# Strassen blocks of a down projection: one ring of five buffers, and the residual added in a later segment

## The chip, the cores and the metric

The kernel runs on one core of one Trainium2 chip. A core has five engines that work side by side and wait for each other through semaphores: TensorE (PE, matrix multiplies, results in PSUM), VectorE (DVE), ScalarE (ACT), GpSimd (POOL) and SyncE (SP). Here SP and POOL mostly start transfers (DMA). The metric is the device time of one execution in microseconds (us); lower is better.

## The reference

One layer of an encoder for two groups of 256 tokens (512 tokens together), model width 2048, in float32:

```python
h = h + mixed                                   # attention and delta-rule heads, projected by w_out
hn = rmsnorm(h, norm_ffn_w)
h = h + (jax.nn.silu(hn @ w_gate) * (hn @ w_up)) @ w_down      # D_FF = 5632
y = rmsnorm(h, final_norm_w)
```

Only the end matters here: the product with `w_down` (5632 x 2048), the residual `h` that is added to it, and the final norm.

## The kernel before

**Layout.** Everything is kept transposed: 128 rows of features on the partitions, the 512 tokens along the free dimension. `hT0` and `hT1` together hold the 16 row tiles of the result of the down projection; `hcol(j)` is a pair of them (128 x 1024), `hrow(i)` a single one. The 5632 rows of the hidden layer are 44 tiles, or 22 pairs, or 11 segments of four tiles. Before the down projection they lie in DRAM as 22 pairs (`s_act`), except segment 9, which stays in SBUF (`sA`); the residual lies there as `s_h2`.

**Precision.** A float32 weight tile is split into two parts that TensorE takes at full rate: ACT writes the rounded part `w_hi` (L134), DVE the rest `w_lo` (L135). Activations are split in the same way. All matmuls stand in a helper, so their line is always L82.

**Plain segments.** `down(s, a)` multiplies a segment: for each of eight columns j it loads a weight tile `w_raw` (L142, SP), splits it, runs 24 matmuls into two PSUM banks, and adds these to `hcol(j)` (L1140). The first segment copies instead (L1138), and after each column adds the residual by a transfer of POOL that accumulates into `hcol(j)` (`plus`, L967).

**Strassen groups.** 14 of the 22 pairs are multiplied in two groups of seven pairs (1792 rows). A group is eight blocks, and each block (`block`, also used by gate and up) makes one `hcol(j)` out of a 2 x 2 split of the weights (W11, W21, W12, W22, each 128 x 896 here) with seven products of 14 matmuls each, instead of eight. The sums of activations that the products need (`xd`) are made once for a group by `combine`: it loads a pair as `raw_a` (L1107, POOL), forms four differences and sums in `cmd` (L1108 to L1110, DVE), and splits both into `xd`. The seven combines run beside the first seven columns of the plain segment that comes before the group (`beside`).

The sums of weights are made in two buffers. SP loads W12 into `w_second` (L977) and W11 into `w_first` (L978); POOL adds W22 and W12 to them by accumulating transfers (L967). W11, W21 and W22 are also loaded as such (`b11`, `b21`, `b22`, L983 to L985, on the page all `b`). The seven products come in this order: b11 (PSUM bank ps_a), second (ps_c), first (ps_d), b21 (ps_a), first + b22 (ps_b; the sum is made in place by DVE, L1016), b22 (ps_d), first + b21 (ps_c; L1028). So `w_second` is last read by the second product's split, `w_first` by the last one's. The results go through `p1`, `p7` and `u2` into the block's output `out` (128 x 1024, L949 to L953, L1021, L1022), which DVE then adds to `hcol(j)` (L1149).

**Buffers.** In the pool `fq` of the down projection, `w_first` and `w_second` have a buffer each. A ring of three buffers of 4 KB a partition (`ring`) serves `raw_a`, `cmd`, `out` and, at the end, a part of the result. Gate and up alternate between two pools, each with its own `w_first` and `w_second`. The b tiles and `w_raw` share a ring of three; `w_hi` and `w_lo` have three each.

**Order of work.** The order of the matmuls is written out. All else is ordered by a planner before the kernel runs: each engine and each queue gets a fixed order, ranked by place in the program. `high_priority` moves instructions ahead in this ranking: by 120 instructions (`AHEAD`) for the splits of weights, by 360 for the loads and additions of `w_first`, `w_second` and the b tiles. A load whose buffer isn't free waits at the head of its queue, and what stands behind it on that queue waits too.

**The course of the down projection:** the plain segment 9 (with the combines of group 0 beside it and the residual added); `load_act` of segment 7, which loads two `raw_a` tiles (L1119, POOL) and splits them into the single buffer `sA`; group 0; the plain segment 7 (combines of group 1); `load_act` of segment 8; group 1; `load_act` of segment 10 into a buffer of its own; the plain segment 8; then segment 10 in two halves of tokens (`finish`), with the final norm.

Of the kernel before, what the change touches and what calls it, by code (L numbers as in the profile page):

```python
# [8 lines left out]
F32 = mybir.dt.float32  # L9
# [9 lines left out]
P = 128  # L19
# [14 lines left out]
GROUP = 7  # L34
NGROUP = 2
SEG0 = NGROUP * GROUP // 2
FIRST_SEG, MID_SEG, LAST_SEGS = 9, 7, (8, 10)
# [32 lines left out]
def hybrid_encoder(ctx: ExitStack, tc: tile.TileContext, xT, w_in, w_ba, w_out, w_gate,  # L70
# [153 lines left out]
    def sm_tile():  # L224
        return psm.tile([P, T], F32, tag="s", name="ps_s")
# [429 lines left out]
    state = {}  # L655
# [199 lines left out]
    pairs = [i for j in range(8) for i in (j, j + 8)]  # L855
# [37 lines left out]
    XC = [hp.tile([P, 7, 2, L], F32R, tag=f"xc{k}", name="xc") for k in range(8)]  # L893
    ga_cm = tc.tile_pool(name="gA", bufs=1, side="left", reuse_waits="tile")
    gA = ga_cm.__enter__()
    acc = gA.tile([P, T], F32, tag="acc", name="ssq_acc2")
    A11, S3, S1, A12, S2, S4, A22 = range(7)
    for n, i in enumerate(pairs):
        j = i % 8
# [62 lines left out]
    def ahead():  # L962
        return tc.high_priority(offset=AHEAD)

    def plus(dst, src):

        nc.gpsimd.dma_start(dst, src, accum_op=ALU.add)  # L967

    def block(w4, pool, xc, ix, p1_pool, new_out, opened=None):


        n = len(xc)
        w11, w21, w12, w22 = w4
        with tc.high_priority(offset=3 * AHEAD):
            first = pool.tile([P, n, P], F32, tag="first", name="w_first")
            second = pool.tile([P, n, P], F32, tag="second", name="w_second")
            nc.sync.dma_start(second, w12)  # L977
            nc.sync.dma_start(first, w11)  # L978
            plus(second, w22)
            plus(first, w12)  # L980
            b11, b21, b22 = [wp.tile([P, 8, P], F32, tag="raw", bufs=3, name=nm)[:, :n]
                             for nm in ("b11", "b21", "b22")]
            nc.sync.dma_start(b11, w11)  # L983
            nc.sync.dma_start(b21, w21)
            nc.sync.dma_start(b22, w22)  # L985

        def bank(pool_, tag, nm):
            return pool_.tile([P, T], F32, tag=tag, name=nm).rearrange("p (a t) -> p a t", a=2)

        pa, pb = bank(pg, "g", "ps_a"), bank(pso, "o0", "ps_b")  # L990
        pc, pd = bank(psm, "s", "ps_c"), bank(pso, "o1", "ps_d")
        with ahead():
            w = w_split(b11)
        product(pa, w, xc, ix[A11], True)
        if opened:
            opened()
        fp, out = state["fp"], new_out()
        p1 = p1_pool.tile([P, L], F32, tag="p1", name="p1")
        plus_both(p1, None, pa)
        with ahead():  # L1000
            w = w_split(second)
        product(pc, w, xc, ix[S3], True)
        p7 = fp.tile([P, 2, L], F32, tag="p7", name="p7")
        nc.scalar.copy(p7, pc)
        with ahead():
            w = w_split(first)
        product(pd, w, xc, ix[S1], True)
        if opened:
            token_rstd2()
        tt(p7, pd, p7, ALU.subtract)  # L1010
        with ahead():
            w = w_split(b21)
        product(pa, w, xc, ix[A12], False, True)
        plus_both(out[:, 0], None, pa)
        with ahead():
            tt(first, first, b22, ALU.add)  # L1016
            w = w_split(first)
        product(pb, w, xc, ix[S2], True, True)
        u2 = fp.tile([P, L], F32, tag="u2", name="u2")
        plus_both(u2, p1, pb)  # L1020
        tt(out[:, 3], p7[:, 0], u2, ALU.subtract)  # L1021
        tt(out[:, 3], out[:, 3], p7[:, 1], ALU.add)  # L1022
        with ahead():
            w = w_split(b22)
        product(pd, w, xc, ix[S4], False, True)
        plus_both(out[:, 2], u2, pd, ALU.subtract)
        with ahead():
            tt(first, first, b21, ALU.add)  # L1028
            w = w_split(first)
        product(pc, w, xc, ix[A22], False, True)  # L1030
        plus_both(out[:, 1], u2, pc)
        return out
# [18 lines left out]

    def scaled(src, f, pool, new_out, opened=None):
        w4 = (src[f, 0], src[f, 1], src[f + 1, 0], src[f + 1, 1])
        out = block(w4, pool, XC, range(7), gA, new_out, opened)
        a = out.rearrange("p (f b) t -> p f (b t)", f=2)
        tt(a, a, state["rstd2"][:, None, :].broadcast_to([P, 2, T]), ALU.mult)
        return out
# [28 lines left out]
    def hrow(i):  # L1086
        return hT[i // 8][:, i % 8]
# [7 lines left out]
    fq = ctx.enter_context(tc.tile_pool(name="fq", bufs=1, side="right", reuse_waits="tile"))  # L1095
    state["fp"] = fq
    XD = [hq.tile([P, 7, 2, L], F32R, tag=f"xd{k}", name="xd") for k in range(GROUP)]

    ix = (0, 3, 4, 1, 5, 6, 2)

    def ring(shape, nm):
        return fq.tile([P] + shape, F32, tag="ra", bufs=3, name=nm)

    def combine(p, k):

# [6 lines left out]
        split(x[:, 1:3, 0], x[:, 1:3, 1], raw[:, 2:])  # L1112
        split(x[:, 3:, 0], x[:, 3:, 1], cm)

    def load_act(s, a):

        for i in range(2):
            raw = ring([2 * T], "raw_a")
            nc.gpsimd.dma_start(raw, s_act[2 * s + i])  # L1119
            split(a[:, 0, 2 * i:2 * i + 2].rearrange("p k t -> p (k t)"),  # L1120
                  a[:, 1, 2 * i:2 * i + 2].rearrange("p k t -> p (k t)"), raw)
        return a

    def down(s, a, beside=None, first=False):

        for j in range(8):
            if beside is not None and j < GROUP:
                combine(beside + j, j)
            ps = [pg.tile([P, T], F32, tag="g", name="ps_g"), sm_tile()]
            wh, wl = load_w(w_down[s - SEG0, j], [2, SEG, P])  # L1130
            for i in range(2):
                for k in range(SEG):
                    mm3(ps[i], wh[:, i, k], wl[:, i, k], a[:, 0, k], a[:, 1, k],
                        k == 0, k == SEG - 1)
            for i in range(2):
                hk = hrow(2 * j + i)
                if first:
                    nc.scalar.copy(hk, ps[i])  # L1138
                else:
                    tt(hk, hk, ps[i], ALU.add)  # L1140
            if first:
                plus(hcol(j), s_h2[2 * j:2 * j + 2].rearrange("i p t -> p i t"))

    def down_group(g):
        for j in range(8):
            out = block([w_group[g, j, i] for i in range(4)], fq, XD, ix, fq,
                        lambda: ring([4, L], "out"))
            h4 = hcol(j).rearrange("p i t -> p (i t)")
            tt(h4, h4, out.rearrange("p a t -> p (a t)"), ALU.add)  # L1149

    def down_half(s, aseg, t0, t1, keep):
        for j in range(8):
# [49 lines left out]
        chains.append(final_norm(b, acc))  # L1202

    down(FIRST_SEG, state["sA"], 0, True)
    a = load_act(MID_SEG, state["new_sA"]())
    down_group(0)
    down(MID_SEG, a, GROUP)
    a = load_act(LAST_SEGS[0], state["new_sA"]())
    down_group(1)
    hq_cm.__exit__(None, None, None)  # L1210
    qp = ctx.enter_context(tc.tile_pool(name="qp", bufs=1, side="left", reuse_waits="tile"))
    last = load_act(LAST_SEGS[1], qp.tile([P, 2, SEG, T], F32R, tag="last", name="aq"))
    keep = [qp.tile([P, 8, 2, SEG, P], F32R, tag=f"r{i}", name="wd") for i in range(2)]
    down(LAST_SEGS[0], a)
    for b in range(NB):
        finish(LAST_SEGS[1], last, b, keep)
    while chains:
# [82 lines left out]
```

## Time and profile before

| | |
|---|---|
| median of 3 runs | 2392.71 us (2391.41 to 2395.05) |
| the profiled execution | 2399.09 us, span of the instructions 2397.3 us |
| PE busy | 2307.9 us, 96% of the span |
| DVE busy | 1795.6 us, 75% |
| ACT busy | 1066.1 us, 44% |
| POOL busy | 247.1 us, 10% |
| mean granted TensorE clock | 0.981 |
| HBM traffic | 163 GB/s over the span |

The page's times are from one execution. Matmuls are pipelined and overlap in the records, so that a busy share of 96% is not yet a TensorE at its peak. Busy shares are also averages over stages that have different limits; the down projection is the last 560 us. A row of a timeline gives start, duration, engine, line, operation, output and inputs, and in brackets how long the engine had been idle and what released it. "L142" is a line of the kernel; SPq is SP's queue of transfers. The share of the DMA engines and the granted clock can be had for any stretch of time.

### The profile page before, as it was taken

Reading aid. Unit: us, or ns where it says so; the run is one execution under the profiler, and the core shown is the slowest. Engines: PE = TensorE matmul, PEld = TensorE weight load, DVE = VectorE, ACT = ScalarE, POOL = GpSimd, SP = SyncE. Lnnn points to the kernel's source line nnn. Section 1 sums busy time; section 2 is a strip of 40 time slices with the busy share of each in tenths; the row PEclk is TensorE's granted clock in tenths of the full one; section 3 lists DMA queues with packets and bytes.
Section 4 is the critical chain, followed back from the end, with each engine's and each line's share of the span. In section 5 each row is a group of like instructions: output and inputs, shape, how many; then the busy total and the mean of one; then the engine's idle time right before and its main releaser. Section 6 shows DMA issues by size and latency. Waiting matters only on the chain.

```text
span 2397.3 us, 32437 instructions
## 1 busy us (share of the span) xinstructions
PE 2307.9 (96%) x12316; PEld 1937.9 (81%) x12316; DVE 1795.6 (75%) x2698; ACT 1066.1 (44%) x1626; POOL 247.1 (10%) x350
## 2 busy tenths in 40 slices
PE   9999999999999999999999999999999788998898
PEld 7887778887877788888888888888888677777787
DVE  7644899965656438988888888888887766786676
ACT  6786332343334216544444444444444533443345
POOL 2112100011000001101010101010011200000000
PEclk9999999999999999999999999999999899998999
DMA  5335322374334536776767676777774856655641
GB/s 198 131 113 158 105 100 94 105 172 144 131 116 174 173 119 223 205 204 189 215 185 218 186 214 187 210 205 199 195 191 152 216 135 158 175 164 134 157 140 71
DMA packets 113980, 393.19 MB, mean 164 GB/s; under 512 B 14336, under 2 KB 14800, under 8 KB 112544
## 3 DMA queue, kind: packets, MB, share of 16 engines
q1 hardware_dynamic: 78416, 275.56, 33.7%
q0 software_dynamic: 35408, 115.56, 22.5%
q8 instruction: 97, 1.59, 0.3%
q14 instruction: 59, 0.48, 0.1%
HBM read 355.59 MB, written 35.47 MB: 163 GB/s over the span
## 4 chain that ended last, share of the span: by engine, by line
PE 69%; DVE 12%; DMA 8%; ACT 5%; issue 4%; POOL 0%; SPq 0%; ACTq 0%; DVEq 0%; POOLq 0%
PE ps_g L82 24%; PE ps_d L82 12%; PE ps_a L82 12%; PE ps_c L82 10%; DMA w_first<-in_w_group_dram 6%; PE ps_b L82 5%; DVE w_lo L135 4%; PE ps_s L82 4%; ACT w_hi L134 2%; DMA raw_a<-s_act 2%; PE ps_o L82 1%; DVE cacc L339 1%; DVE prod L550 1%; ACT E L457 1%; DVE W L552 1%
## 5 line engine op out<-in xcount | busy, mean ns | idle before, releaser
L82 PE MATMUL ps_g<-xhi,w_hi 128*128 128x512 f32 x896 | 362.1, 404 | 1.7 <-DVE on L427 1.4
L82 PE MATMUL ps_g<-xhi,w_lo 128*128 128x512 f32 x896 | 351.1, 392 | 2.0 <-DVE w_lo L135 2.0
L82 PE MATMUL ps_g<-xlo,w_hi 128*128 128x512 f32 x896 | 350.6, 391 | 1.1 <-DVE xlo L243 1.1
L134 ACT ACTIVATE w_hi<-w_first 128x1024 fp32r<-128x1024 f32 (+1 forms) x180 | 186.0, 1033 | 364.4 <-DMA w_first<-in_w_group_dram 112.4
L135 DVE TENSOR_TENSOR w_lo<-w_first,w_hi 128x1024 fp32r<-128x1024 f32 (+1 forms) x180 | 214.0, 1189 | 166.4 <-ACT w_hi L134 162.1
L135 DVE TENSOR_TENSOR w_lo<-w_raw,w_hi 128x1024 fp32r<-128x1024 f32 x166 | 202.9, 1223 | 120.2 <-ACT w_hi L134 115.6
L134 ACT ACTIVATE w_hi<-w_raw 128x1024 fp32r<-128x1024 f32 x166 | 175.3, 1058 | 263.2 <-PE ps_g L82 218.2
L134 ACT ACTIVATE w_hi<-b 128x1024 fp32r<-128x1024 f32 (+1 forms) x180 | 186.0, 1033 | 221.5 <-issue 133.4
L82 PE MATMUL ps_a<-xc,w_hi 128*128 128x512 f32 x704 | 251.9, 397 | 1.0
L82 PE MATMUL ps_c<-xc,w_hi 128*128 128x512 f32 x704 | 249.9, 395 | 0.0
L82 PE MATMUL ps_d<-xc,w_hi 128*128 128x512 f32 x704 | 249.9, 395 | 0.0
L135 DVE TENSOR_TENSOR w_lo<-b,w_hi 128x1024 fp32r<-128x1024 f32 (+1 forms) x180 | 213.5, 1186 | 8.8 <-ACT w_hi L134 2.9
L82 PEld LDWEIGHTS ps_g<-xhi,w_hi 128*128 128x128 f32 x896 | 168.8, 188 | 39.5 <-issue 5.9
L82 PEld LDWEIGHTS ps_g<-xhi,w_lo 128*128 128x128 f32 x896 | 168.7, 188 | 39.2 <-DVE w_lo L135 3.3
L82 PEld LDWEIGHTS ps_g<-xlo,w_hi 128*128 128x128 f32 x896 | 169.0, 189 | 35.4 <-DVE xlo L243 2.6
L82 PE MATMUL ps_a<-xc,w_lo 128*128 128x256 f32 x704 | 197.0, 280 | 0.0
L82 PE MATMUL ps_c<-xc,w_lo 128*128 128x256 f32 x704 | 197.0, 280 | 0.0
L82 PE MATMUL ps_d<-xc,w_lo 128*128 128x256 f32 x704 | 196.9, 280 | 0.0
L82 PEld LDWEIGHTS ps_a<-xc,w_hi 128*128 128x128 f32 x704 | 131.9, 187 | 36.7 <-issue 6.1
L82 PEld LDWEIGHTS ps_c<-xc,w_hi 128*128 128x128 f32 x704 | 132.0, 187 | 31.0
L82 PEld LDWEIGHTS ps_d<-xc,w_hi 128*128 128x128 f32 x704 | 132.0, 187 | 30.9
L82 PE MATMUL ps_d<-xd,w_hi 128*128 128x512 f32 x224 | 100.2, 472 | 37.8 <-ACT w_hi L134 36.0
(358 smaller groups left out, 4758.1 us busy)
## 6 DMA issues: line engine op xcount, KB each, us to landing
w_raw<-in_w_in_dram SPq DMA_DIRECT2D x110, 512.0 KB, 3.3
b<-in_w_gate_dram SPq DMA_DIRECT2D x66, 512.0 KB, 4.4
b<-in_w_up_dram SPq DMA_DIRECT2D x66, 512.0 KB, 4.9
b<-in_w_group_dram SPq DMA_DIRECT2D x48, 448.0 KB, 3.9
w_raw<-in_w_out_dram SPq DMA_DIRECT2D x32, 512.0 KB, 3.5
w_raw<-in_w_down_dram SPq DMA_DIRECT2D x32, 512.0 KB, 3.3
w_second<-in_w_gate_dram SPq DMA_DIRECT2D x22, 512.0 KB, 8.4
w_first<-in_w_gate_dram SPq DMA_DIRECT2D x22, 512.0 KB, 5.7
```

What stands on the lines that cost most here:

```text
L82: pin(nc.tensor.matmul(*a, **k))
L134: act(out=hi, in_=src, func=AF.Copy)
L135: tt(lo, src, r32(hi), ALU.subtract)
L339: stt(a3[:, :, lo:hi], x3[:, :, lo + o:hi + o], cw[:, ct, j:j + 1], a3[:, :, lo:hi], ALU.mult, ALU.add)
L457: pin(act(out=E[half[0], s, s:], in_=G[half[0], s:], func=AF.Exp, bias=NG[half[0], s:s + 1]))
L550: tt(pv, W[:, s0:s1, s0:c], kkq[:, c, 0, None, s0:c].broadcast_to([P, n, j]), ALU.mult)
L552: nc.vector.tensor_reduce(W[:, s0:s1, c], pv, AX.X, ALU.add)
```

## The change

`w_first` and `w_second` of the group blocks lose their own buffers. They are drawn from `ring`, which goes from three buffers to five and so holds raw tiles, weight sums and outputs. To that end `block` takes a function that makes the two tiles, instead of a pool; gate and up pass one that does what the pool did. The pool `fq` grows by 1 KB a partition.

`load_act` of segments 7 and 8 no longer stands ahead of a group: its first half comes behind block 2, the second behind block 4, in program order.

The residual is no longer added in the first segment but in the next to last one (segment 8), by the same eight accumulating transfers, each behind its column's additions.

```diff
-    def block(w4, pool, xc, ix, p1_pool, new_out, opened=None):
+    def block(w4, new_w, xc, ix, p1_pool, new_out, opened=None):
...
         with tc.high_priority(offset=3 * AHEAD):
-            first = pool.tile([P, n, P], F32, tag="first", name="w_first")
-            second = pool.tile([P, n, P], F32, tag="second", name="w_second")
+            first, second = new_w("first"), new_w("second")
             nc.sync.dma_start(second, w12)
             nc.sync.dma_start(first, w11)
             plus(second, w22)
...
     def ring(shape, nm):
-        return fq.tile([P] + shape, F32, tag="ra", bufs=3, name=nm)
+        return fq.tile([P] + shape, F32, tag="ra", bufs=5, name=nm)
...
-    def load_act(s, a):
+    def load_act(s, a, pairs=range(2)):
 
-        for i in range(2):
+        for i in pairs:
             raw = ring([2 * T], "raw_a")
             nc.gpsimd.dma_start(raw, s_act[2 * s + i])
...
-    def down(s, a, beside=None, first=False):
+    def down(s, a, beside=None, first=False, residual=False):
...
-            if first:
+            if residual:
                 plus(hcol(j), s_h2[2 * j:2 * j + 2].rearrange("i p t -> p i t"))
 
-    def down_group(g):
+    def down_group(g, s):
+
+        a = state["new_sA"]()
         for j in range(8):
-            out = block([w_group[g, j, i] for i in range(4)], fq, XD, ix, fq,
+            out = block([w_group[g, j, i] for i in range(4)],
+                        lambda nm: ring([GROUP, P], "w_" + nm), XD, ix, fq,
                         lambda: ring([4, L], "out"))
             h4 = hcol(j).rearrange("p i t -> p (i t)")
             tt(h4, h4, out.rearrange("p a t -> p (a t)"), ALU.add)
+            if j in (2, 4):
+                load_act(s, a, [j // 4])
+        return a
...
     down(FIRST_SEG, state["sA"], 0, True)
-    a = load_act(MID_SEG, state["new_sA"]())
-    down_group(0)
+    a = down_group(0, MID_SEG)
     down(MID_SEG, a, GROUP)
-    a = load_act(LAST_SEGS[0], state["new_sA"]())
-    down_group(1)
+    a = down_group(1, LAST_SEGS[0])
...
-    down(LAST_SEGS[0], a)
+    down(LAST_SEGS[0], a, residual=True)
```

More of the change, by code (lines that the diff above doesn't have):

```diff
@@ L1053, in scaled @@
         w4 = (src[f, 0], src[f, 1], src[f + 1, 0], src[f + 1, 1])
-        out = block(w4, pool, XC, range(7), gA, new_out, opened)
+        out = block(w4, lambda nm: pool.tile([P, 8, P], F32, tag=nm, name="w_" + nm), XC,
+                    range(7), gA, new_out, opened)
         a = out.rearrange("p (f b) t -> p f (b t)", f=2)
```

## The prediction

> **What bounds the kernel now.** I read the page first, then the busy times by stretch, the waits of TensorE and last the timeline of one block.
>
> ```profile
> PEclk9999999999999999999999999999999899998999
> PE ps_g L82 24%; PE ps_d L82 12%; PE ps_a L82 12%; PE ps_c L82 10%; DMA w_first<-in_w_group_dram 6%; PE ps_b L82 5%; DVE w_lo L135 4%; PE ps_s L82 4%; ACT w_hi L134 2%; DMA raw_a<-s_act 2%; PE ps_o L82 1%; DVE cacc L339 1%; DVE prod L550 1%; ACT E L457 1%; DVE W L552 1%
> ```
>
> The chain that ended last is TensorE nearly all the way, but its largest piece of another kind is the load of w_first from the group weights, a tile that only the 16 Strassen blocks of the down projection use. The granted clock dips in the last part alone. So I cut that part by stage; columns: microseconds, busy time of PE, PEld, DVE, ACT, POOL, then granted clock, DMA share, GB/s.
>
> ```profile
> 1500.00:1540.00 40.00, 40.00 (x228) 34.64 (x227) 34.05 (x45) 18.20 (x22) 4.01 (x5) 1.00 0.77 213
> ...
> 1837.00:1880.50 43.50, 43.50 (x194) 36.05 (x193) 23.60 (x34) 19.68 (x30) 11.21 (x13) 1.00 0.92 248
> 1880.50:2074.00 193.50, 156.13 (x780) 130.46 (x779) 132.68 (x187) 72.29 (x100) 19.35 (x23) 0.89 0.62 156
> ...
> 2119.00:2293.40 174.40, 152.28 (x785) 128.42 (x784) 123.08 (x170) 62.28 (x83) 13.18 (x16) 0.92 0.57 145
> 2293.40:2337.00 43.60, 43.60 (x195) 36.09 (x194) 30.16 (x34) 16.51 (x16) 0.00 (x0) 1.00 0.43 146
> ```
>
> The first row lies in gate/up, whose blocks are built by the same helper from two pairs of weight buffers: TensorE never rests. Rows two and five are plain down segments (first and next to last). Rows three and four are group 0 and group 1, eight blocks each: TensorE rests and its clock falls to 0.89 and 0.92. Here is where one block loses its time: the timeline, and under it the chain of waits.
>
> ```profile
> 2198.31 1.09 DVE L135 TENSOR_TENSOR w_lo<-w_first,w_hi 128x896 fp32r<-128x896 f32 x1 [1.73 <-ACT w_hi L134]
> ...
> 2199.43 0.33 SPq L978 DMA_DIRECT2D w_first<-in_w_group_dram  x1
> ...
> 2203.68 0.89 POOL L967 DMA_DIRECT2D w_first<-in_w_group_dram  x1 [15.20 <-DVE out L953]
> ...
> 2204.61 0.40 PE L82 MATMUL ps_a<-xd,w_hi 128*128 128x512 f32 x1
> ...
> 2205.73 1.22 DVE L1149 TENSOR_TENSOR hT<-hT,out 128x1024 f32<-128x1024 f32 x1
> ...
> 2209.44 0.28 PE L82 MATMUL ps_c<-xd,w_lo 128*128 128x256 f32 x1
> ...
> 2210.04 0.95 ACT L134 ACTIVATE w_hi<-w_first 128x896 fp32r<-128x896 f32 x1 [6.87 <-DMA w_first<-in_w_group_dram]
> ...
> 2211.04 0.49 PE L82 MATMUL ps_d<-xd,w_hi 128*128 128x512 f32 x1 [1.33 <-ACT w_hi L134]
> ```
>
> ```profile
> 2203.68 6.25 DMA w_first<-in_w_group_dram
> ...
> 2211.02 1.10 DVE w_lo L135
> 2212.17 4.01 PE ps_d L82 x13
> ...
> 2288.57 2.42 PE ps_d L82 x14
> 2291.00 2.43 PE ps_c L82 x14
> ```
>
> There is one buffer for w_first. Its last reader ends at 2199.40, the reload is issued at 2199.43, W12 is added into it by a second transfer at 2203.68, and only after ACT and DVE have split it can the third product run in full, at 2212.17. TensorE had been ready at 2209.7: 2.5 us are lost but for one matmul, and the 13 matmuls that follow take 4.01 us where an undisturbed 14 take 2.43. By 13/14 of 2.43 that is another 1.8 us, which the list of waits doesn't hold:
>
> ```profile
> PE ps_d L82 <- ACT w_hi L134: 36.0, 13, 4.7
> PE ps_a L82 <- DVE xd L135: 12.8, 3, 6.7
> ```
>
> So a block that never waits takes 7 x 2.43 = 17.0 us, eight take 136, and the groups lose 193.5 - 136.1 = 57.4 and 174.4 - 136.1 = 38.3 us: 95.7 us is the most this change can touch.
>
> **The ring in steady state.** Every block draws first (F), second (S) and the output (O) from five buffers. I take it that slots are handed out in the order in which tiles are created, each tile getting whichever of the five comes free first. The trace bears out the order:
>
> ```profile
> 1850.31 0.33 SPq L142 DMA_DIRECT2D w_raw<-in_w_down_dram  x1
> ...
> 1861.66 0.33 SPq L983 DMA_DIRECT2D b<-in_w_group_dram  x1
> ```
>
> Block 0's b tiles have a head start of 360 instructions, more than the distance to the last w_raw of the stage (some 40 instructions), share w_raw's ring, and still come behind it. In a block of 17.0 us, S comes free about when the block starts (its split runs just ahead of its product), F at 11.8 (the 2199.40 above is 5.2 us before the next block's 2204.61), O at 19.3 (2205.73 + 1.22 is 2.3 us into the next block). Going through the ring, F of block j+2 gets F of block j's release (at 11.8), S of j+2 gets S of j+1's (17.0), O of j+2 gets O of j's (19.3). F is then wanted at 2 x 17.0 + 4.9 = 38.9 and S at 36.4: 27 and 19 us of lead. What such a load takes:
>
> ```profile
> w_second<-in_w_group_dram SPq DMA_DIRECT2D x16, 448.0 KB, 5.9
> ...
> w_second<-in_w_group_dram POOLq DMA_DIRECT2D x16, 448.0 KB, 4.9
> ```
>
> 5.9 + 4.9, with 1.0 for ACT's and 1.1 for DVE's split: 13 us. So the wait of blocks 1 to 7 goes: group 0 from block 1 on and group 1 from block 1 on hold about 38 us of loss each. SP's queue is in order; a load that waits there holds up the b loads behind it, but with these leads none waits long. What is late next? DVE: 123.08 / 8 = 15.4 us a block, 90% of 17.0, against 34.05 / 40 = 85% in gate/up, where TensorE never rests. DMA: 145 GB/s x 174.4 / 139 = 182 GB/s, below the 213 of gate/up. I leave 0.5 us a block, 7 us in all, for what this tightness costs (bounds 0 and 1.5 us a block).
>
> **The raw tiles in the ring.** load_act moves behind blocks 2 and 4. Its two loads pass on POOL between the additions; its splits cost
>
> ```profile
> L135 DVE TENSOR_TENSOR aA<-raw_a,aA 128x1024 fp32r<-128x1024 f32 x2 | 2.4, 1223 | 3.1 <-ACT aA L134 3.1
> ```
>
> 1.2 us of DVE each, within the slack. Each raw tile puts the ring one place back until it is split: the S two blocks on gets its slot some 15 us before use instead of 19, still over 13. I take 1 us for each of the four (bounds 0 and 7.2, worked out under the rivals).
>
> **The start of a group.** This is where the change costs something. F and S of block 0 had buffers of their own and were loaded early; now they stand in the ring behind the 14 raw and cmd tiles of the seven combines. On the other hand combines get five slots instead of three, and in the first segment POOL no longer puts the residual in front of them:
>
> ```profile
> 1855.84 0.69 DVE L1108 TENSOR_TENSOR cmd<-raw_a 128x512 f32<-128x512 f32 x1 [5.56 <-DMA raw_a<-s_act]
> ...
> 1899.86 1.22 DVE L135 TENSOR_TENSOR xd<-cmd,xd 128x1024 fp32r<-128x1024 f32 x1
> ```
>
> ```profile
> 1881.92 1.19 POOL L967 DMA_DIRECT2D hT<-s_h  x1 [5.55 <-ACT hT L1138]
> 1882.72 0.98 POOL L1107 DMA_DIRECT2D raw_a<-s_act  x1
> ```
>
> Before, the combines end at 1901.1, while TensorE is through with the segment at 1880.5. DVE is busy 23.60 of 43.50 us there, so the seven could be done by 1881 if the raw tiles came in time; I take 1884 (bounds 1880 and 1901). S of block 0 gets the slot of the sixth raw tile. In the segment of group 1, where DVE sets the pace, that was
>
> ```profile
> 2109.16 0.70 DVE L135 TENSOR_TENSOR xd<-raw_a,xd 128x512 fp32r<-128x512 f32 x1
> ...
> 2117.91 1.23 DVE L135 TENSOR_TENSOR xd<-cmd,xd 128x1024 fp32r<-128x1024 f32 x1
> ```
>
> 9.3 us before the last split (2109.86 to 2119.1). With 13 us for the load S is ready 3.7 us after the last combine, TensorE wants it after 2.4: 1.3 us late, 3 with the slow clock behind it. In group 0's crowded stretch a load takes longer:
>
> ```profile
> hT<-s_h POOLq DMA_DIRECT2D x8, 512.0 KB, 7.8
> ...
> w_second<-in_w_group_dram SPq DMA_DIRECT2D x2, 448.0 KB, 5.7
> w_second<-in_w_group_dram POOLq DMA_DIRECT2D x2, 448.0 KB, 7.5
> ```
>
> 5.7 + 7.5 + 2.1 = 15.3, ready 6.0 after, 3.6 late, 5.4 with the slow clock. The blocks after them begin, before the change, at
>
> ```profile
> 1917.89 0.40 PE L82 MATMUL ps_a<-xd,w_hi 128*128 128x512 f32 x1
> ...
> 2137.24 0.39 PE L82 MATMUL ps_a<-xd,w_hi 128*128 128x512 f32 x1
> ```
>
> Block 0 of group 0 now ends at 1884 + 17.0 + 5.4 = 1906.4 instead of 1917.9: a loss of 9 instead of 20 us. Group 1's first block takes 17.0 + 3 against 18.2 (from 2119.0): 1.8 us worse, 3 us of loss.
>
> On the slow clock the Trainium skill ("TensorE: Matmul & The Clock Gate", Part 1) says that the clock halves after an idle window of about 3.4 us and comes back after as long a busy one. Here gaps of 1.3 and 0.6 us around one matmul were enough, so the measurement decides; by the page's window the two late starts might keep their clock, and the sum would be some 3 us lower.
>
> **The residual.** Its eight additions (7.8 us from issue to landing) leave the first segment and come behind the columns of the next to last. POOL is idle there (0.00 in the row above), and the last segment reads column j only after all eight columns of this one. The last addition is issued after 2337 and lands by 2346; the last segment's first half takes 27 us for its eight columns, so it reaches the last one after some 24 us:
>
> ```profile
> 2336.97 27.35 PE ps_g L82 x228
> ```
>
> I cost it at nothing; were the cover gone, 7.8 us once.
>
> **The sum.** What is left of the 95.7: 9 + 3 at the starts, 7 for tightness, 4 for the raw tiles = 23. The gain is 73 us. The profiled execution took 2399.1 us around its span of 2397.3; 2399.1 - 73 = 2326. The median of the runs is 6.4 lower: 2320.
>
> **The rivals.** First, a **new wait in the ring**: slots go round strictly, each tile waiting for the one five places before it. Without raw tiles nothing changes; but with one in between, S of blocks 3 and 5 would wait for F of the block before, which is free at 11.8. It would be ready at 11.8 + 13 = 24.8 and is wanted at 19.4: 5.4 us, 7.2 with the clock, four times: 29 us instead of 4, 2345. The same size comes out if **DVE sets the pace** at 85% as in gate/up: 15.4 / 0.85 = 18.1 us a block, 1.1 more in 16 blocks, 18 instead of 7, 2331. For it speaks 90%; against it, that DVE has no work then that TensorE waits for.
>
> Second, **no gain**: the transfers themselves set 145 to 156 GB/s, and loads that start earlier land no earlier. 2393. Against it speak 213 and 248 GB/s in the other rows.
>
> Third, **slower**: the ring is clogged. If at the time when S of the next block needs a slot two of the five are still held (a raw tile, an O that waits for its addition), S waits in every block for F's last split, and takes the place of F as the load on the path: 24.2 us a block by the sum above. Blocks 1 to 7 take 22.4 now ((2074 - 1917.9) / 7 is 22.3), so 14 x 1.8 = 25 us more, less 10 at the starts: 2408. It decides from two slots held at 11.8 us on. Against it: O is free 2.3 us after its block.
>
> **How the numbers follow.** Forecast 0.62, the milder gain of the first rival 0.23, no gain 0.06, slower 0.09. A measurement of this kernel tells 0.2%, 4.8 us, from no change. Faster 0.85, same 0.06, slower 0.09. The likeliest's own range is 2300 (all but 3 us of the 95.7 gone) to 2340. The whole range goes up to 2370, the first rival with the first segment's combines as late as before (17 us).
>
> **What would show it.** The reload L978 is issued a block earlier than it is used and TensorE's wait before ps_d for w_hi is gone; group blocks take 17 to 18 us at a clock of 1.00; block 0 waits for w_second in ps_c; combines of the first segment end near 1884; the additions into hT stand behind 2230. I am wrong if SP waits for out or w_first before L977 in most blocks, or if ps_a waits for xd as long as before.

## The result, and the profile after

The changed kernel is slower: 2408.1 us median (2400.3 to 2411.75, six runs) against 2392.26 us (2390.36 to 2397.41) for the kernel before on the same chip, a ratio of 1.0058 [1.0039, 1.0077]. The forecast was 2320.

The profiled execution took 2404.1 us (span 2402.3), one of the quicker ones; before it was 2399.1 (span 2397.3). What follows explains these 5 us. That the medians lie 16 apart, and not 5, is scatter between executions that no profile here resolves.

The page's rows after, that answer to the two shown of before (granted clock in 40 slices, and the chain of waits by line):

```profile
PEclk9999999999999999999999999999999989999899
PE ps_g L82 21%; PE ps_c L82 13%; PE ps_d L82 12%; PE ps_a L82 11%; PE ps_b L82 6%; DMA w_second<-in_w_group_dram 5%; PE ps_s L82 5%; DVE w_lo L135 4%; ACT w_hi L134 2%; DVE prod L550 2%; DVE W L552 2%; PE ps_o L82 1%; DVE cacc L339 1%; DMA w_first<-in_w_group_dram 1%; ACT E L457 1%
```

The load of w_first went from 6% of the chain to 1%; the load of w_second came up to 5% in its place. One load has taken the place of the other. Group 0, group 1 and segment 8 after (columns as in the prediction: microseconds, busy PE, PEld, DVE, ACT, POOL, granted clock, DMA share, GB/s):

```profile
1881.30:2069.80 188.50, 155.89 (x785) 131.24 (x784) 123.09 (x169) 66.23 (x87) 14.31 (x19) 0.89 0.53 143
...
2113.40:2297.40 184.00, 154.71 (x785) 130.65 (x784) 122.39 (x169) 64.44 (x83) 14.22 (x18) 0.91 0.53 146
2297.40:2341.00 43.60, 43.60 (x195) 36.11 (x194) 27.78 (x32) 14.64 (x14) 7.58 (x7) 1.00 0.85 214
```

Cut further at the first ps_a matmul of each block, the two executions compare so (us):

| stage | before | after | difference |
|---|---|---|---|
| up to the first segment | 1837.0 | 1837.9 | +0.9 |
| first segment | 43.5 | 43.4 | -0.1 |
| group 0, block 0 | 37.4 | 21.3 | -16.1 |
| group 0, blocks 1 to 7 | 156.1 | 167.2 | +11.1 |
| segment 7 | 45.0 | 43.6 | -1.4 |
| group 1, block 0 | 18.2 | 18.2 | 0 |
| group 1, blocks 1 to 7 | 156.2 | 165.8 | +9.6 |
| the rest | 103.9 | 104.9 | +1.0 |

So the gain at the start of group 0 came, and more of it than forecast. The 14 inner blocks, which were to fall from 22.3 to 17.5 us, rose to 23.8. TensorE's largest wait in the two groups, which was in ps_d for the split of w_first (36.0 us, 13 times), is now in ps_c for that of w_second:

```profile
PE ps_c L82 <- ACT w_hi L134: 53.9, 15, 5.2
```

Here is one of the blocks, as a timeline (block 1 of group 0 runs from 1902.56 to 1925.42; the last row is the second product of block 2):

```profile
1916.83 1.09 DVE L135 TENSOR_TENSOR w_lo<-b,w_hi 128x896 fp32r<-128x896 f32 x1 [0.23 <-ACT w_hi L134]
...
1917.95 0.33 SPq L983 DMA_DIRECT2D b<-in_w_group_dram  x1
...
1918.33 0.42 SPq L976 DMA_DIRECT2D w_second<-in_w_group_dram  x1
1918.34 0.37 ACT L949 COPY out<-ps_a 128x256 f32<-128x256 f32 x1 [1.54 <-PE ps_a L82]
...
1918.85 0.38 SPq L977 DMA_DIRECT2D w_first<-in_w_group_dram  x1
...
1923.04 0.87 POOL L967 DMA_DIRECT2D w_second<-in_w_group_dram  x1 [18.81 <-DVE w_lo L135]
...
1930.37 0.95 ACT L134 ACTIVATE w_hi<-w_second 128x896 fp32r<-128x896 f32 x1 [8.72 <-DMA w_second<-in_w_group_dram]
...
1931.37 0.80 PE L82 MATMUL ps_c<-xd,w_hi 128*128 128x512 f32 x1 [3.37 <-ACT w_hi L134]
```

And the chain of waits through the same place:

```profile
1923.04 7.23 DMA w_second<-in_w_group_dram
...
1932.50 4.42 PE ps_c L82 x13
```

The split of b22 ends at 1917.92 and frees a b buffer. At once SP issues three loads: b21 (L983), then w_second (L976) and w_first (L977) of the next block. That is 15.8 us into the block. From there the load takes 4.7 us, the accumulating one 7.2, the splits 2.1, so that TensorE has w_second's parts at 1932.50, 7.08 us into block 2, where an undisturbed block wants them after 2.43. With 13 matmuls in 4.42 instead of 2.26 us this makes 17.0 + 4.65 + 2.16 = 23.8 us a block.

What held up L976 is told by SP's list of waits over both groups (line, releaser: us in total, times, longest). After:

```profile
SPq L983 <- DVE w_lo L135: 230.6, 15, 18.8
SPq L142 <- DVE w_lo L135: 48.1, 7, 16.3
```

The first row of the same list of the kernel before:

```profile
SPq L984 <- DVE w_first L1028: 186.4, 14, 15.6
```

L976 and L977 don't stand in the list of after: they waited for no buffer. It is b21's load in front of them that waits, 15.4 us in each of 15 blocks. It waited before as well (L984 there), but w_second's load then stood ahead of it. (w_first's stood behind it before too; its own buffer came free later still: in the block that the prediction shows, b21's load left at 2194.82 and w_first's at 2199.43.) The Trainium skill, "DMA: Bandwidth & Descriptors", section "Anatomy of one DMA — SWDGE (gpsimd) path", says that a wait on a semaphore happens on the issuing sequencer ahead of the dispatch and not in the DMA engines. That section is about transfers of GpSimd; the rows of SP's queue agree: b21's load is issued 0.03 us after the split ends, and the two behind it follow within 1.3 us.

Why the loads changed places is seen in the planned order. Instructions are numbered in it; for each tile stand the first instruction that uses it, the tile that had its buffer before, and that tile's last use (rows of other tiles left out). The changed kernel, group 0:

```
first use  tile           buffer from   last used
15952      b21 (j+1)      b22           15942
15955      out (j)        w_second      15731
15965      w_second (j+1) w_first       15813
15979      w_first (j+1)  out           15877
...
16109      b21            b22           16099
16112      out            w_second      15887
16123      w_second       out           16034
```

A block is 157 numbers long. The buffers for w_second and w_first had been out of use for 90 to 150 numbers, more than half a block; b21's had been used ten numbers earlier. But w_second comes right behind the first use of the output of the block before, in every block of both groups. My reading, the **order theory**, is this: the ring gives out its places in the program's order of first use, whatever head start `high_priority` gives; an output is first written only behind the fourth product (L949); the two weight tiles of the next block, which the program uses after it, can therefore not be planned before that write, and there SP's next instruction is a b21 load that has yet to wait. (First use, and not creation: w_first is created ahead of w_second, but loaded after it, and in the table it stands behind it. No run separates the two further.)

### The profile page after: what moved, and what is told of

The parts are those of the page before. It is cut to its first block, busy times and chain, and to the rows that moved or that the text cites. A ratio compares the mean times of both kernels' runs of the same rounds, so it can differ in the third digit from the quotient of the medians.

```text
span 2402.3 us, 32408 instructions
## 1 busy us (share of the span) xinstructions
PE 2309.1 (96%) x12316; PEld 1940.6 (81%) x12316; DVE 1793.2 (75%) x2698; ACT 1065.9 (44%) x1626; POOL 246.3 (10%) x350
## 3 DMA queue, kind: packets, MB, share of 16 engines
q0 software_dynamic: 35408, 115.56, 22.4%
## 4 chain that ended last, share of the span: by engine, by line
PE 69%; DVE 15%; DMA 7%; ACT 5%; issue 4%; SPq 0%; POOL 0%; ACTq 0%; DVEq 0%; POOLq 0%
PE ps_g L82 21%; PE ps_c L82 13%; PE ps_d L82 12%; PE ps_a L82 11%; PE ps_b L82 6%; DMA w_second<-in_w_group_dram 5%; PE ps_s L82 5%; DVE w_lo L135 4%; ACT w_hi L134 2%; DVE prod L550 2%; DVE W L552 2%; PE ps_o L82 1%; DVE cacc L339 1%; DMA w_first<-in_w_group_dram 1%; ACT E L457 1%
## 5 line engine op out<-in xcount | busy, mean ns | idle before, releaser
L82 PE MATMUL ps_c<-xd,w_hi 128*128 128x512 f32 x224 | 105.0, 491 | 53.9 <-ACT w_hi L134 53.9
```

Of the source, the lines that this page charges most:

```text
L82: pin(nc.tensor.matmul(*a, **k))
```

## The experiments

All kernels compute the whole result. The first four ask what keeps the loads late. Against the order theory stand: that five buffers are too few, that the moved steps (residual, load_act) cost the time, and that it is SP's queue as such.

**Sums first.** The loads of w_first and w_second become a helper `sums`, called for block j+1 just ahead of block j's output; in the ring they then come before it. The edit, shortened:

```diff
-            out = block([w_group[g, j, i] for i in range(4)],
-                        lambda nm: ring([GROUP, P], "w_" + nm), XD, ix, fq,
-                        lambda: ring([4, L], "out"))
+        def new_out(j):
+            fetch(j + 1)             # ready.append(sums(...)), two tiles of the ring
+            return ring([4, L], "out")
+        fetch(0)                     # ahead of the loop
+            out = block(..., ready.pop(0), XD, ix, fq, lambda: new_out(j))
```

> The changed kernel, but the two weight sums of block j+1 are created (and their loads issued) ahead of the output of block j; ring of five, residual and load_act as changed. Order theory: in the changed kernel a tile gets its place in the ring in the order of first use, so the sums of block j+1 stand behind the output of block j, which is first written only after the fourth product. With the order turned round they are loaded a block ahead: group blocks 17 to 18.5 us instead of 23.8, 14 blocks, so some 80 us less than the changed kernel's 2408: 2315 to 2340. Rival, five buffers are too few: blocks stay above 21 us, 2375 or more. Rival, the moved steps (residual, load_act) cost the time: 2395 to 2410.

Measured: 0.9661 [0.9638, 0.9685], 2318.7 us, within 2 us of the forecast for the change itself. The two groups in stages, each divided behind block 0:

```profile
1878.80:1902.70 23.90, 20.63 (x99) 17.18 (x98) 15.23 (x20) 9.66 (x13) 2.07 (x3) 0.86 0.75 185
1902.70:2023.90 121.20, 121.20 (x688) 105.15 (x687) 107.42 (x150) 56.60 (x74) 12.52 (x16) 1.00 0.70 185
2067.50:2087.40 19.90, 17.59 (x100) 15.00 (x99) 13.71 (x20) 8.52 (x11) 0.92 (x2) 1.00 0.72 175
2087.40:2206.20 118.80, 118.80 (x687) 104.74 (x687) 107.43 (x150) 55.82 (x72) 12.50 (x16) 1.00 0.72 191
```

Blocks 1 to 7 take 17.3 and 17.0 us: TensorE is busy throughout and its clock 1.00. Five buffers, both moved steps and the raw tiles in the ring are all still there.

**A ring for the outputs.** The same memory, parted: three buffers for raw tiles and sums, two for outputs.

```diff
-        return fq.tile([P] + shape, F32, tag="ra", bufs=5, name=nm)
+        return fq.tile([P] + shape, F32, tag="ra", bufs=3, name=nm)
-                        lambda: ring([4, L], "out"))
+                        lambda: fq.tile([P, 4, L], F32, tag="ro", bufs=2, name="out"))
```

> The changed kernel, but the outputs have a ring of their own of two buffers, and the other ring has three: five buffers as before, fewer for the weight sums. Order theory: with no output ahead of them in the ring the sums are loaded early again, blocks 17 to 19 us, 2315 to 2350. Rival, five buffers are too few: with three for sums and raw tiles it gets worse, 2408 or more. Rival, the moved steps cost the time: 2395 to 2410.

Measured: 0.9701 [0.9678, 0.9725], 2327.0 us; blocks 1 to 7 take 17.0 to 18.5 us. Three buffers for the loads are enough once no output stands between them: "too few" falls.

**The moved steps alone.** w_first and w_second get their own buffers back, the ring three; residual and load_act stay where the change put them.

```diff
-        return fq.tile([P] + shape, F32, tag="ra", bufs=5, name=nm)
+        return fq.tile([P] + shape, F32, tag="ra", bufs=3, name=nm)
-                        lambda nm: ring([GROUP, P], "w_" + nm), XD, ix, fq,
+                        lambda nm: fq.tile([P, GROUP, P], F32, tag=nm, name="w_" + nm), XD, ix, fq,
```

> The two moves alone: w_first and w_second keep a buffer each and the ring three, as before the change; the residual comes in segment 8 and load_act behind blocks 2 and 4. Order theory: the wait for w_first is there as before (blocks of some 22 us), the combines of the first segment are no longer held by the residual's additions (some 10 us less in block 0 of group 0), the end is 1 us longer: 2378 to 2392. Rival, the moved steps cost the time: 2400 to 2412.

Measured: 0.996 [0.994, 0.998], 2388.9 us. TensorE's first wait over the down projection is again that of the kernel before, in ps_d for the single w_first:

```profile
PE ps_d L82 <- ACT w_hi L134: 36.4, 13, 4.7
```

The moves are worth a little by themselves; without the ring of five they cost nothing.

**The sums on ACT's queue.** For the group blocks ACT issues the two loads instead of SP.

```diff
-            nc.sync.dma_start(second, w12)
-            nc.sync.dma_start(first, w11)
+            q = nc.scalar if n == GROUP else nc.sync
+            q.dma_start(second, w12)
+            q.dma_start(first, w11)
```

> The changed kernel, but the loads into w_first and w_second of the group blocks are issued on ACT's queue instead of SP's. Order theory: on ACT's queue they stand behind the copy into the output of the block before, which runs about 16 us into the block, when SP issues them in the changed kernel too: no change, 2398 to 2414. Rival, they are late only because they stand behind the waiting load of b21 on SP's queue: blocks 17 to 19 us, 2315 to 2350.

Measured: 1.0015 [1.0002, 1.0027], 2401.4 us. No b21 stands ahead of them on this queue, and still they come late, right behind the copy that first writes the output:

```profile
1920.38 0.37 ACT L949 COPY out<-ps_a 128x256 f32<-128x256 f32 x1 [1.23 <-PE ps_a L82]
1920.39 0.33 ACTq L977 DMA_DIRECT2D w_second<-in_w_group_dram  x1
```

That is the planned place itself. So two things must come together: the plan puts the loads behind the output's first write, and something on their own queue, there, holds them (on SP a b21 load, on ACT the copy).

**The ring alone.** Both moves are undone, the ring of five stays as changed. The edit, shortened (group 1 alike):

```diff
-            if residual:
+            if first:
...
-            if j in (2, 4):
-                load_act(s, a, [j // 4])
...
-    a = down_group(0, MID_SEG)
+    a = load_act(MID_SEG, state["new_sA"]())
+    down_group(0)
```

> The ring of five with the order of use as changed, but both moves undone: residual in the first segment, load_act ahead of the groups. Order theory: blocks of 23 to 24 us as in the changed kernel, and the starts of the groups later by what the two moves save with the sums created first (9 and 6 us): 2410 to 2426. Rival, the moves make the changed kernel slow: 2395 or less.

Measured: 0.9935 [0.9912, 0.9959], 2387.7 us: my expectation missed, by over 20 us, and the time lies in the rival's range. The stages of this run tell why: group 0 from block 1 on, then the whole of group 1.

```profile
1924.40:2050.60 126.20, 121.30 (x688) 106.18 (x687) 102.06 (x147) 57.21 (x73) 11.86 (x15) 0.97 0.72 183
2094.20:2282.80 188.60, 157.25 (x786) 131.94 (x785) 122.67 (x169) 64.65 (x83) 14.20 (x18) 0.88 0.53 138
```

One group runs free (blocks 2 to 7 take 17.0 us; block 1 still took 24.3) and the other as in the changed kernel, with the same code and without either move. SP's queue in a block of group 0 (1946) and of group 1 (2137), all in one view, the timeline:

```profile
1946.14 0.33 SPq L982 DMA_DIRECT2D b<-in_w_group_dram  x1
1946.52 0.43 SPq L976 DMA_DIRECT2D w_second<-in_w_group_dram  x1
...
1958.60 0.33 SPq L983 DMA_DIRECT2D b<-in_w_group_dram  x1
...
2137.69 0.33 SPq L982 DMA_DIRECT2D b<-in_w_group_dram  x1
2155.78 0.33 SPq L983 DMA_DIRECT2D b<-in_w_group_dram  x1
2156.16 0.43 SPq L976 DMA_DIRECT2D w_second<-in_w_group_dram  x1
```

In group 0 w_second leaves right behind b11 and b21 comes last, 12 us later; in group 1 b21 comes first, waits 18 us, and w_second behind it. The planned order says the same (first use):

```
group 0:  15976 out   15977 w_second   15991 w_first   16005 b21
group 1:  17746 b21   17749 out        17759 w_second  17772 w_first
```

In both w_second stands right behind the output. b21's load falls 28 places behind it in the one and 13 ahead of it in the other, and with that 6.6 us a block. This sharpens the theory: standing behind the output's first write does no harm on SP by itself (SP doesn't wait for ACT's copy); it lets b21 slip ahead. I had taken the slow order as certain for this ring, and it is one of two: group 1 gets it with the moves and without, group 0 only with them. So the rival is right for group 0, in so far as the moves tip the planner into the slow order there (what in them does it stays open), and wrong for group 1.

**A touch.** The changed kernel as it is, but each group output is written early: one column is cleared on DVE when the tile is created, behind the first product. 16 small instructions more; nothing else differs.

```diff
         fp, out = state["fp"], new_out()
+        if n == GROUP:
+            nc.vector.memset(out[:, 0, :1], 0.0)
```

> The changed kernel with one addition: the moment a group block's output is created, one column of it is set to zero by DVE (it is overwritten later), so that its first use in the planned order comes a product and a half earlier. Order theory, sharpened: the sums of the next block are planned right behind the first use of this output, and on SP's queue that was just behind b21 of the next block, which waits for a buffer until late in the block. With the earlier first use they are planned ahead of b21, nothing else being changed; all 16 blocks then run as those of group 0 did in the ring alone, 17 to 18 us: 2315 to 2335. Rival, the blocks of group 0 in the ring alone were fast because no raw tiles stood between them: those behind blocks 2 and 4 stay slow, 2345 or more.

Measured: 0.9709 [0.9683, 0.9735], 2324.1 us: 16 clears, which compute nothing, turn 2408 into 2324. SP's queue in a block of group 0, and under it the whole of group 0:

```profile
1916.93 0.33 SPq L982 DMA_DIRECT2D b<-in_w_group_dram  x1
1919.52 0.33 SPq L976 DMA_DIRECT2D w_second<-in_w_group_dram  x1
1921.73 0.33 SPq L977 DMA_DIRECT2D w_first<-in_w_group_dram  x1
1928.91 0.33 SPq L983 DMA_DIRECT2D b<-in_w_group_dram  x1
```

```profile
1881.20:2025.00 143.80, 139.52 (x786) 120.10 (x785) 123.06 (x179) 67.63 (x91) 14.25 (x19) 1.00 0.72 186
```

This settles the cause: with the same ring, the same moves and the same queue, an earlier first write of the output brings the loads ahead of b21, and all but one of the blocks behind block 0 to 17.0 to 18.2 us. (Block 0 takes 21.1 and 23.1 us.) The one, in group 1, took 22.9 us. There the chain goes through the load of a raw tile, and not of a sum; the splits planned behind this tile's come late:

```profile
2103.66 7.70 DMA raw_a<-s_act
```

So the rival has a part in that block; those beside the other three raw tiles take 18.2 us at most.

The others measure the smaller terms, all on top of "sums first", whose ratio was 0.9661 [0.9638, 0.9685].

**The residual first again** (added in the first segment, as before the change):

```diff
-            if residual:
+            if first:
                 plus(hcol(j), s_h2[2 * j:2 * j + 2].rearrange("i p t -> p i t"))
```

> The kernel with the sums created first (2318.7 us), but the residual added in the first segment again. Contention theory: in segment 8 the residual's transfers take DMA time from the weight loads of the last two segments (7.4 us to land instead of 3.3), and TensorE waits 4 to 6 us around the last segment; that goes, and block 0 of group 0 becomes later again because POOL's queue holds the raw tiles behind the additions, by some 8 to 12 us: 2320 to 2328. Rival, the cover at the end holds (the move costs nothing there): block 0 alone, 2326 to 2332.

Measured: 0.9715 [0.9698, 0.9731], 2327.6 us. The time lies in both ranges; the stages decide for the contention. Block 0 of group 0 takes 40.1 us instead of 23.9 (more than the 8 to 12 that I expected), about as before the change (37.4), while the end from segment 8 on takes 104.2 instead of 109.5. So the move earns 16 us at one place and pays 5 at the other. What it pays for is seen in segment 8 (37 us of it), without the additions in this run and with them in the changed kernel:

```profile
2223.00:2260.00 37.00, 37.00 (x165) 30.65 (x164) 24.94 (x28) 12.02 (x13) 0.00 (x0) 1.00 0.46 150
```

```profile
2300.00:2337.00 37.00, 37.00 (x165) 30.65 (x164) 22.76 (x25) 11.09 (x11) 7.30 (x6) 1.00 0.85 204
```

54 GB/s more take the DMA engines from 0.46 to 0.85 busy. The median w_raw load, from issue to landing, takes 3.3 us without them (first row, this run) and 5.5 with them (second, the changed kernel; both over segments 8 and 10):

```profile
w_raw<-in_w_down_dram SPq DMA_DIRECT2D x16, 512.0 KB, 3.3
```

```profile
w_raw<-in_w_down_dram SPq DMA_DIRECT2D x16, 512.0 KB, 5.5
```

**load_act ahead of the groups again** (shortened; group 1 alike):

```diff
-            if j in (2, 4):
-                load_act(s, a, [j // 4])
...
-    a = down_group(0, MID_SEG)
+    a = load_act(MID_SEG, state["new_sA"]())
+    down_group(0)
```

> The kernel with the sums created first, but load_act of segments 7 and 8 stands ahead of the groups again. If its place matters, two raw tiles in front of the first sums in the ring make block 0 of each group later by 3 to 6 us: 2322 to 2332. If its place in the groups costs something instead (raw tiles in the ring between the blocks), the time falls below 2316; no difference if DVE and the ring have room either way: 2316 to 2321.

Measured: 0.9703 [0.9688, 0.9717], 2325.1 us. Block 0 takes 27.2 and 24.6 us, against 23.9 and 19.9: two more raw tiles ahead of its sums. This move was worth 8 us at the two starts.

**Block 0's sums earlier:** created ahead of the sixth of the seven combines.

```diff
+            if beside is not None and j == GROUP - 2:
+                fetch(beside // GROUP, 0)
```

> The kernel with the sums created first, and the sums of block 0 are created before the sixth combine instead of after the seventh. If they are late in block 0 only because they stand behind all the raw and cmd tiles in the ring, TensorE's wait before ps_c in block 0 of both groups goes (23.9 and 19.9 us become 18 to 19 and 17.5): 2309 to 2314. Rival, three slots left for the last two combines make xd late instead: 2317 to 2325.

Measured: 0.9646 [0.9628, 0.9664], 2311.2 us, the lowest median of all. Block 0 takes 20.8 and 18.5 us, against 23.9 and 19.9; about 2 and 1 us more than I expected. The interval overlaps that of "sums first", so the step between the two isn't shown by the times; the blocks' lengths speak for it.

**The residual in group 1**, one addition behind each block; that in segment 8 goes:

```diff
+            if g:
+                plus(hcol(j), s_h2[2 * j:2 * j + 2].rearrange("i p t -> p i t"))
```

> The kernel with the sums created first, but the residual is added in group 1, one column behind each block, instead of in segment 8. Contention theory: the last two segments get their weight loads undisturbed again and the 4 to 6 us there go; the blocks of group 1 have DMA time to spare (182 and then some 212 GB/s): 2312 to 2316. Rival, the additions hold up POOL's queue or the loads in group 1: its blocks exceed 17.5 us, 2320 or more.

Measured: 0.9657 [0.9639, 0.9676], 2314.5 us. The end falls from 109.5 to 103.7 us, but group 1 rises from 138.8 to 143.2. Of these 4.4 us, 1.7 are in block 0, ahead of the first addition, and 2.0 in one later block (19.0 us): how much of it is the transfers' isn't shown.

**Both of the last two** edits together:

> The sums of the next block created first, the sums of block 0 created before the sixth combine, and the residual added in group 1: the two last gains together. If they add up (7.5 and 4.2 us below 2318.7): 2304 to 2310. If the end of the kernel waits for something else once group 1 is shorter: 2311 or more.

Measured: 0.9645 [0.9617, 0.9674], 2314.9 us, on a chip where the kernel before took 2403. The ratio is that of "block 0's sums earlier" alone; my expectation that the two gains add up missed. The version to keep is that one, or "sums first", which the intervals don't tell from it: some 3.5% faster than the kernel before, and 4% faster than the changed one.

## Why the prediction was wrong, step by step

- **What bounds the kernel: right.** The reload of w_first into its only buffer was what could be gained. The span of "sums first" lies 81.6 us below that of the kernel before (2397.3 - 2315.7), out of the 95.7 that the prediction gave as the most.
- **The ring in steady state: this step failed.** It took slots to be handed out in the order of creation as soon as one comes free, worked out leads of 27 and 19 us from that, and said that "with these leads none waits long". The slots were free in time, as worked out; but a free slot isn't an issued load. In the plan the loads stand behind the output's first write, and on SP behind b21: in the block shown w_second's left 15.8 us into the block ahead and TensorE had it 4.65 us late; the 14 inner blocks took 23.8 us instead of 17.5. The step asked what stands behind the load of w_first on SP, and not what stands ahead of it. The row that it took as evidence of the order (b behind w_raw) was of another ring and could not test a tile that is first written late. And a row that would have warned was there in the profile of before: SP stood 186.4 us at b21's load (L984), 13 us a block, so whatever stands behind that load leaves late.
- **The tightness and the raw tiles: put too high, once the order is mended.** They were put at 0.5 us a block and 1 us a raw tile; with "sums first" blocks run at 17.3 us in group 0 and 17.0 in group 1, so both terms together took about 2 us, not 11. DVE at 90% of a block's time doesn't set the pace: TensorE has no idle time in the rows of these blocks.
- **The starts: right, somewhat better.** The last combine was taken to end at 1884 and ended at 1882.8; TensorE began the group at 1881.3 and didn't wait for it. Block 0 was to take 22.4 and 20.0 us and took 21.3 and 18.2. The row of the last combine after:

```profile
1881.56 1.23 DVE L135 TENSOR_TENSOR xd<-cmd,xd 128x1024 fp32r<-128x1024 f32 x1 [1.13 <-ACT xd L134]
```

- **The residual: mis-sized.** It was costed at nothing, with POOL's idleness as the cover. POOL only issues the transfers; what they share is the DMA engines, with the w_raw loads. In the kernel that waits in every block it cost 1 us (103.9 to 104.9); where the blocks run free, 5 to 6 (109.5 against 104.2 and 103.7). The bound of 7.8 held. It still pays, since the combines gain 16.
- **The sum: close for a kernel in which the loads do leave early.** 73 us were forecast, "sums first" gains 3.4% [3.15, 3.62], 81 us of 2392. It is the changed kernel that doesn't do it. That "sums first" came within 2 us of the forecast is partly luck: some 9 us too much for tightness and raw tiles stand against 5 to 6 us for the residual that were put at nothing.
- **The rivals.** In "sums first", which has the same ring, strict slots (2345), DVE as the pace (2331) and "no gain" (2393) all fall: its blocks 1 to 7 take 17.0 to 17.3 us, those behind a raw tile too, and its group 1 moves 189 GB/s over its 138.7 us. The third had the place of the load right (w_second on the path instead of w_first), its price (24.2 us a block; 23.8 measured) and the time (2408). Its holder is wrong: the ring was not clogged, no load of a sum waited for a slot, and what it waited for was b22's split by way of b21's load. That 2408 was met to the microsecond is partly chance: of the blocks' loss and the start's gain both came out otherwise than it put them (after the table, +20.7 and -16.1, where it had +25 and -10).
- **What would show it.** SP's queue ahead of L977 was the right place to look; the line that waits there is b21's, for `w_lo`, and not a sum's for `out` or `w_first`. TensorE's wait before ps_d did go, as the prediction asked, and came back before ps_c in every inner block.

## What to carry to other kernels

Where tiles of several kinds share a ring, count not only the buffers but ask in which order places are given out and what stands ahead of each load on its queue: here a tile that is first written late held back the loads that the program puts after that write, although their buffers were free. Putting the loads ahead of that tile, or writing one column of it early, was worth 3.5 to 4% here, where the change itself moved 0.6%. And a transfer that is added "beside idle work" has to be held against what else uses the DMA engines there, not against the engine that issues it.

## What the runs showed of the hardware

**Accumulating transfers load the DMA engines far beyond their bytes.** The queues in segment 8 of the changed kernel (2297 to 2345; packets, MB, share of the engines' time; q0 is POOL's with the additions, q1 SP's with the w_raw loads):

```profile
q0 software_dynamic: 1782, 3.45, 45.9%
q1 hardware_dynamic: 1791, 6.48, 38.2%
```

The additions are 35% of the bytes and 54% of the busy share, 2.3 times as much for a byte, and a w_raw load beside them takes 5.5 us instead of 3.3. Their packets are half as large here, but that isn't all: in "sums first", 2123 to 2138, where both queues load tiles of 448 KB, POOL's additions are 0.92 MB in 35.9% of the time and SP's loads 2.22 MB in 40.8%, a factor of 2.1.

**The half clock after a gap isn't a matter of the gap's length alone.** Two starts of a block, each with one matmul between two gaps (timeline, gaps in the brackets; then the row of the chain for the 13 matmuls that follow). "Sums first", group 1, 2.3 us of gaps in all, and the 13 at full rate:

```profile
2071.77 0.50 PE L82 MATMUL ps_c<-xd,w_hi 128*128 128x512 f32 x1 [1.68 <-ACT w_hi L134]
2072.90 0.38 PE L82 MATMUL ps_c<-xd,w_lo 128*128 128x256 f32 x1 [0.62 <-DVE w_lo L135]
```

```profile
2072.90 2.48 PE ps_c L82 x13
```

The changed kernel, group 0, 1.9 us of gaps, and the 13 take 3.99 us:

```profile
1885.24 0.49 PE L82 MATMUL ps_c<-xd,w_hi 128*128 128x512 f32 x1 [1.31 <-ACT w_hi L134]
1886.36 0.58 PE L82 MATMUL ps_c<-xd,w_lo 128*128 128x256 f32 x1 [0.63 <-DVE w_lo L135]
```

```profile
1886.36 3.99 PE ps_c L82 x13
```

The prediction put 1.8 us of slow clock behind every such start; so it is there behind some and not behind others. The Trainium skill ("TensorE: Matmul & The Clock Gate", Part 1) has a window of 3.4 us that runs freely, so that it matters where in it a gap falls. The traces agree: in all 13 the granted clock changes only at steps of 3.41 us, on a grid that runs on through the down projection. Here are such steps (columns as above; in so short a stretch the DMA share can pass 1), first of the changed kernel, then of "sums first":

```profile
1882.89:1886.30 3.41, 1.53 (x7) 0.81 (x6) 1.51 (x2) 1.22 (x2) 0.00 (x0) 1.00 0.72 132
1886.30:1889.71 3.41, 3.35 (x10) 2.88 (x11) 1.91 (x3) 1.79 (x2) 0.00 (x0) 0.50 0.02 5
```

```profile
2068.65:2072.06 3.41, 1.73 (x10) 1.17 (x8) 0.31 (x1) 0.95 (x1) 0.86 (x1) 1.00 1.07 209
2072.06:2075.47 3.41, 2.79 (x16) 2.28 (x16) 2.32 (x3) 2.11 (x4) 0.00 (x0) 1.00 1.08 211
```

In the changed kernel both gaps fell into one step: TensorE was busy for 1.53 of its 3.41 us, and the next step ran at half the clock, long enough for most of the 13 matmuls. In "sums first" the longer gap ended up in one step and the shorter in the next: 1.73 and 2.79 us busy, and the clock stayed. Over the 13 traces, from 1800 to 2290 us, all 69 steps at full clock in which TensorE was busy for less than 0.445 of the time were followed by one at half clock, and none of the 1514 with more than 0.55; in between both occur (21 steps, 0.45 and 0.51 here among them). A step that is idle as a whole, as the same part of the skill has it, was not needed: the measurement decides.
